# A two-level Strassen MLP kernel: blocked layout of w1 with shorter loads, eight w2 sums one superblock later, an own order for the last pair

## The chip, the cores and the metric

The kernel runs on one core of one Trainium2 chip. The metric is the device time of one execution in microseconds (us).

## The reference

A transformer MLP without biases, on 8 x 1024 tokens, all arrays float32:

```
x:  (8, 1024, 1024)     w1: (1024, 4096)     w2: (4096, 1024)
h = x @ w1
h = 0.5 * h * (1 + tanh(sqrt(2 / pi) * (h + 0.044715 * h ** 3)))
return h @ w2
```

## The kernel before, in words

**Tiling.** The 8192 tokens are worked in eight superblocks of 1024. In each, the first matrix product (x @ w1, "m1") is followed by gelu and the second (@ w2, "m2"). Both products are computed with seven block products in place of eight (Strassen's scheme in Winograd's form): each operand is cut into four blocks "11", "12", "21", "22", sums of blocks are made (`W_SUM`, products 5, 6, 7, 4; products 1, 2, 3 take raw blocks, `W_TERM`), and the seven results are added up in PSUM and by VectorE. Superblocks 0 and 1 use one level of this; superblocks 2 to 7 use two, so that each first-level product is itself made of seven second-level ones. All matmul operands are float16; all of VectorE's sums go through one helper, `tt` (line 149).

**What superblocks 0 and 1 do besides.** Superblock 0 casts w1 and w2 from float32 and keeps the float16 blocks in DRAM (`w1_d`, `w2_d`). Superblocks 0 and 1 also make the sums of weights that the later superblocks will load: the first-level sums of w1 by quads of columns (`MadeQuad.sum`, jobs "q"), their second-level sums (`MadeQuad.inner_sums`), the first-level sums of w2 (jobs "w"), and the second-level sums of w2 (`split_jobs`, jobs "p": job p26 is sum 6 of product 2; each job is two VectorE sums of 128 x 1024 and one 512 KB store into `in_d`, issued by GpSimd at line 967). Which job runs behind which tile of the second product is written out by hand in the table `FILL`, one entry for superblock 0 and one for superblock 1: the key "52" is the third tile of product 5. The order of products is 1, 2, 5, 6, 3, 7, 4. Jobs "g" are sums of gelu's outputs, jobs "x" sums of the next superblock's x, jobs "i" second-level sums (of w1's first quad in superblock 0, of x in superblock 1). The function `ahead` inside `matmul1` does the same for the first product: which w1 sums are made while which pair of column chunks is multiplied.

VectorE, like each engine, runs its instructions in program order. The adds that take a product's tile out of PSUM (`post`) stand on VectorE between these jobs.

**Superblocks 2 to 7, first product.** `matmul1_late` walks over eight pairs of column chunks, j = 0 to 7, and each pair's operands are one half of a w1 quad, `StoredHalf(0)` to `StoredHalf(7)`. A half is loaded from `w1_d` by SyncE in up to six transfers (line 295), one for each entry of `GROUPS`: operands 1 and 5; their second-level sums s1 and s5; 2 and s2; 6 and s6; 3 and s3; 7 and 4. A transfer carries 128 rows of 4096 bytes, 512 KB. For halves 3 to 7 s1 and s5 are not loaded but made by GpSimd in `make` (line 320, four sums of 128 x 512), from operands 1 and 5. Of half 0 no second-level sums of products 1, 5 and 6 are used, since products 1, 5 and 6 of pair 0 are made whole (`Pair.whole`). The halves 0 and 1 are requested in the second product of the superblock before, the others pair by pair in `matmul1_late`, three ahead. At most eight transfers are outstanding on SyncE's queue.

The order of steps in a pair is written out by hand: `PAIR` interleaves the first steps of pair j with the last steps of pair j−1 (keys with a prime), and `PAIR_FIRST` is the order for pair 0. Behind the eighth pair the primed keys of `PAIR` run by themselves; this is called the drain here. The kinds of key: `m31` is second-level product 1 of first-level product 3 (line 711, `Pair.part`, 256 columns); `h40` is half 0 of product 4, made whole (line 499, `product`, 512 columns, where `matmul1` multiplies as well); `z`, `e`, `f`, `s`, `u` are VectorE adds; `c`, `a`, `p` are copies by ScalarE; `g110` is a gelu; `d` is the difference g21 − g22 or like it (`difference`, line 518, on GpSimd, for the last pair on VectorE); `i35` is a second-level sum of x. `X_SUMS` says behind which keys of pair 1 the remaining x sums are made.

**Superblocks 2 to 7, second product.** `matmul2` uses `Inner` for each first-level product (line 1016); its w2 sums come from `in_d` and `w2_d` by SyncE. In superblocks 0 and 1 the second product's matmuls are at line 1057 (`matmuls2`).

**Layout of w1.** A w1 tile of a quad has [128 partitions, 2 halves x 4 row chunks, 256 columns]; the second-level block of a row chunk and a column chunk is a set of strided runs of 128 columns, and a chunk of columns is `[:, :, c]` with a stride.

Of the kernel before, what the change touches and what calls it, by code (L numbers as in the profile page):

```python
# [14 lines left out]
P = 128  # L15
# [19 lines left out]
m11 i35 m21 m14 a0 i55 m25 a1 m51 p0 i65 e21 m61 i15 z21  # L35
""".split()
# [16 lines left out]
def slots(table):  # L53
# [32 lines left out]
def kernel(  # L86
# [74 lines left out]
    def halves(t):  # L161
        return t.rearrange("p (h k) n -> p h (k n)", h=2)
# [22 lines left out]
    def columns(t, c, n=1):  # L185

        h, c = divmod(c, 2)
        return t[:, h * KH:(h + 1) * KH, c * P:(c + n) * P]
# [11 lines left out]
    class MadeQuad:  # L200


        def __init__(self, q, first, store):
            self.q, self.first, self.store = q, first, store
            self.raw = {b: unit(2 * KH, 2 * P) for b in BLOCKS}
            self.ops = {m: self.raw[b] for m, b in W_TERM.items()}
            if not first:
                for b in ("12", "11", "22", "21"):
                    nc.sync.dma_start(out=halves(self.raw[b]), in_=w1_at(q, term.get(b, b)))

        def load(self):

            for b, t in self.raw.items():
                k0 = (int(b[0]) - 1) * KH
                halves = t.rearrange("p (h k) n -> p k h n", h=2)
                for k in range(0, KH, 2):
                    cast_in(
                        halves[:, k:k + 2],
                        w1v[int(b[1]) - 1, :, k0 + k:k0 + k + 2, self.q * QW:(self.q + 1) * QW],
                        pool_copy,  # L220
                        view=lambda st: st.rearrange("p k (h n) -> p k h n", h=2),
                    )

        def load_cols(self, b, c, n, cast):
# [9 lines left out]
            def casts():  # L234
                for k, st, cast in staged:
                    for a in range(k // KH, (k + kn) // KH):
                        tc.keep_in_program_order(cast(
                            out=columns(self.raw[f"{a + 1}{b + 1}"], c, n),
                            in_=st[:, a * KH - k:(a + 1) * KH - k, :],
                        ))  # L240
# [3 lines left out]
        def sum(self, m, cols=None, pin=False):  # L244
            if m not in self.ops:
                self.ops[m] = self.raw["12"] if m == 7 and not self.first else unit(2 * KH, 2 * P)
# [9 lines left out]
        def inner_sums(self, m):  # L256
            t = self.ops[m].rearrange("p (h k c) (e n) -> p h k c e n", h=2, k=2, e=2)
            s = up.tile([P, 2, 4, 2, P], DT, name="u")

            def operand(b):  # L260
                if isinstance(b, int):
                    return s[:, :, list(S_SUM).index(b)]
                return t[:, :, int(b[1]) - 1, :, int(b[0]) - 1, :]
# [15 lines left out]
    class StoredHalf:  # L279


        def __init__(self, i, room=()):
# [3 lines left out]
            for ks in GROUPS:  # L286
# [7 lines left out]
                if two is not None:  # L294
                    nc.sync.dma_start(
                        out=two[:, :len(ks)].rearrange("p e n -> p (e n)"),
                        in_=w1_d[q, ks][:, h].rearrange("p e n -> p (e n)"),
                    )

        def two(self, ks):  # L300
            two = self.room.pop(0) if self.room else up.tile([P, 2, KH * 2 * P], DT, name="u")
            for e, m in enumerate(ks):
                if isinstance(m, str):
                    self.sums[int(m[1])] = two[:, e].rearrange("p (j c n) -> p j c n", j=4, c=2)
                else:
                    self.ops[m] = two[:, e].rearrange("p (k n) -> p k n", k=KH)
            return two

        def make(self):
            s = self.two(("s1", "s5")).rearrange("p e (j c n) -> p e j c n", j=4, c=2)  # L310
            t = self.both.rearrange("p e (k c r n) -> p e k c r n", k=2, c=2, r=2)

            def operand(b):
                if isinstance(b, int):
                    return s[:, :, list(S_SUM).index(b)]
                return t[:, :, int(b[1]) - 1, :, int(b[0]) - 1, :]
# [6 lines left out]
        def chunk(self, m, c):  # L323
            return self.ops[m][:, :, c % 2 * P:(c % 2 + 1) * P]

    class XOps(dict):
# [20 lines left out]
        def inner_sum(self, m, j):  # L347
# [3 lines left out]
            def operand(b):  # L351
                if isinstance(b, int):
                    return self.inner[m][:, SUMS.index(b)]
                k, t = int(b[0]) - 1, int(b[1]) - 1
# [178 lines left out]
    def matmul1(xs, sb, quads, start=None):  # L533
# [5 lines left out]
        def ahead(j):  # L539

            if j // 2 == NI // QC - 1:
                return ()
            q, second = divmod(j, 2)
            if not second:
# [5 lines left out]
            quad = quads[q + 1]  # L550
            if sb == 0:
                return [lambda m=m: quad.sum(m, pin=True) for m in SUMS] if second else ()
# [116 lines left out]
    class Pair:  # L669
# [21 lines left out]
        def part(self, m, i):  # L691
# [8 lines left out]
            for k in range(2):  # L700
                if i in S_TERM:
                    r, o = (int(d) - 1 for d in S_TERM[i])
                    w = ops[:, 2 * o + k, r * P:(r + 1) * P]
                else:
                    w = self.source.sums[m][:, list(S_SUM).index(i), k, :]
                if i in W_TERM:
                    o, t = (int(d) - 1 for d in W_TERM[i])
                    x = xs[m][:, 2 * o + k, t * HT // 2:(t + 1) * HT // 2]
# [56 lines left out]
    def matmul1_late(xs, sb, quads, g):  # L765
# [10 lines left out]
        for j in range(n + 1):  # L776
            if MADE_HALF <= j + 1 < n:
                quads[j + 1].make()
            if j < n:
                quads += [StoredHalf(i) for i in range(len(quads), min(j + 3, n))]  # L780
                now = Pair(j, quads[j], xs, g)
            for key in PAIR if j else PAIR_FIRST:
# [4 lines left out]
                elif j < n:  # L787
                    now.run(key)
# [3 lines left out]
            if j == n:  # L792
                break
# [400 lines left out]
```

## Time and profile before

| | us |
|---|---|
| median of three timed runs | 1492.52 |
| the three | 1492.61, 1492.52, 1486.17 |
| the profiled execution's own time | 1490.02 |
| its span in the profile | 1488.2 |
| TensorE busy in it | 1460.1 |
| VectorE busy | 1263.1 |
| ScalarE busy | 612.2 |
| GpSimd busy | 457.1 |

The stages in the profiled execution, read from the timeline of TensorE, in us from the start of the span: superblock 0's first product ends at about 113 and its second at 215; superblock 1's end at 313 and 410; superblock 2's at 500 and 592; each later superblock takes about 180; the span ends at 1488.

How to read it: PE is TensorE, DVE VectorE, ACT ScalarE, POOL GpSimd, SP SyncE. A row of a timeline has the start, the duration, the engine, the line, the operation with its output and inputs by the program's names and their shape, how many of them in a row, and in brackets the idle time before the first of them and what ended it. Names such as `u`, `gc`, `g` and `tmp` are pools of tiles: `u` holds weights and x, `g` and `gc` gelu's outputs and their sums, `tmp` partial results in float32, `ps` PSUM banks. A row of waits has the engine's line, the releaser, and the total, the count and the longest wait. Durations of matmuls overlap, so that two in a row start closer together than they last.

### The profile page before, as it was taken

Reading aid. Unit: us, or ns where it says so; the run is one execution under the profiler, and the core shown is the slowest. Engines: PE = TensorE matmul, PEld = TensorE weight load, DVE = VectorE, ACT = ScalarE, POOL = GpSimd, SP = SyncE. Lnnn points to the kernel's source line nnn. Section 1 sums busy time; section 2 is a strip of 40 time slices with the busy share of each in tenths; the row PEclk is TensorE's granted clock in tenths of the full one; section 3 lists DMA queues with packets and bytes.
Section 4 is the critical chain, followed back from the end, with each engine's and each line's share of the span. In section 5 each row is a group of like instructions: output and inputs, shape, how many; then the busy total and the mean of one; then the engine's idle time right before and its main releaser. Section 6 shows DMA issues by size and latency. Waiting matters only on the chain.

```text
span 1488.2 us, 28427 instructions
## 1 busy us (share of the span) xinstructions
PE 1460.1 (98%) x10635; PEld 1038.2 (70%) x10635; DVE 1263.1 (85%) x2226; ACT 612.2 (41%) x1226; POOL 457.1 (31%) x473
## 2 busy tenths in 40 slices
PE   8999989999999999999999999999999999999998
PEld 4444434444477788778876788777886778867787
DVE  5657648757789999999998999999999999999987
ACT  5566016631067411663126721366213762156510
POOL 1542222212346012560026501264012731136111
PEclk9999999999999999999999999999999999999999
DMA  9999998887899999999999999999999999997896
GB/s 325 342 352 399 269 362 315 276 264 247 345 342 236 325 325 374 370 233 364 301 370 341 226 372 306 360 349 226 380 332 351 321 276 337 348 377 237 311 303 214
DMA packets 205706, 472.69 MB, mean 318 GB/s; under 512 B 75648, under 2 KB 80768, under 8 KB 204672
## 3 DMA queue, kind: packets, MB, share of 16 engines
q1 hardware_dynamic: 177632, 373.35, 73.7%
q0 software_dynamic: 27936, 97.53, 21.9%
q8 instruction: 83, 1.36, 0.4%
q14 instruction: 55, 0.45, 0.1%
HBM read 370.15 MB, written 115.34 MB: 326 GB/s over the span
## 4 chain that ended last, share of the span: by engine, by line
PE 81%; DVE 7%; DMA 7%; issue 2%; SPq 2%; POOL 1%; POOLq 0%; DVEq 0%
PE ps L1016 32%; PE ps L499 21%; PE ps L711 17%; PE ps L1057 10%; DMA u<-w_d 5%; DVE tmp L149 2%; DVE ps L149 2%; SPq L173 2%; DVE u L149 2%; DMA g<-w_d 2%; DVE gc L149 1%; PE ps L432 1%; POOL u L320 1%; DMA gc<-in_w_dram 1%; POOL xb L474 0%
## 5 line engine op out<-in xcount | busy, mean ns | idle before, releaser
L149 DVE TENSOR_TENSOR tmp<-tmp,ps 128x256 f32<-128x256 f32 (+1 forms) x582 | 312.9, 555 | 94.1 <-PE ps L499 38.6
L499 PE MATMUL ps<-u 128*128 128x512 f16 x1552 | 364.2, 379 | 2.7 <-DVE u L149 1.8
L176 ACT COPY tmp<-ps 128x512 f32<-128x512 f32 (+1 forms) x398 | 208.7, 541 | 301.2 <-PE ps L1057 148.1
L149 DVE TENSOR_TENSOR ps<-tmp,ps 128x256 f32<-128x256 f32 x720 | 293.2, 425 | 34.2 <-PE ps L711 24.7
L711 PEld LDWEIGHTS <-u 128*128 128x128 f16 x2688 | 263.3, 98 | 80.8 <-DMA u<-w_d 6.2
L1016 PE MATMUL ps<-u,gc 128*128 128x256 f16 x2592 | 290.8, 273 | 0.0
L1016 PEld LDWEIGHTS <-gc 128*128 128x128 f16 x2592 | 253.6, 98 | 29.4
L149 DVE TENSOR_TENSOR u<-u 128x2048 f16<-128x2048 f16 (+3 forms) x320 | 231.9, 768 | 31.1 <-DMA u<-w_d 15.1
L499 PEld LDWEIGHTS <-u 128*128 128x128 f16 x1552 | 151.6, 98 | 151.0 <-issue 5.4
L512 ACT ACTIVATE g<-ps 128x512 f16<-128x512 f32 x326 | 190.0, 594 | 118.5 <-PE ps L711 71.2
L711 PE MATMUL ps<-u 128*128 128x256 f16 x1520 | 229.6, 274 | 0.0
L1016 PE MATMUL ps<-u,g 128*128 128x256 f16 x2016 | 227.9, 273 | 0.0
L176 ACT COPY u<-ps 128x512 f32<-128x512 f32 (+1 forms) x134 | 77.9, 586 | 353.2 <-PE ps L1016 345.6
L826 POOL DMA_DIRECT2D out_dram<-u x70 | 63.8, 955 | 488.1 <-DVE u L149 251.4
L1016 PEld LDWEIGHTS <-g 128*128 128x128 f16 x2016 | 197.3, 98 | 22.8
L711 PE MATMUL ps<-gc,u 128*128 128x256 f16 x1168 | 194.9, 274 | 9.4 <-DMA u<-w_d 5.1
L149 DVE TENSOR_TENSOR u<-u,ps 128x512 f32<-128x512 f32 x216 | 147.8, 684 | 37.1 <-PE ps L1016 29.0
L1057 PE MATMUL ps<-u,g 128*128 128x512 f16 x768 | 168.1, 381 | 3.8 <-DVE tmp L149 3.8
L518 POOL TENSOR_TENSOR g<-g,g 128x1024 f16<-128x1024 f16 x42 | 89.2, 2124 | 202.8 <-ACT g L512 202.8
L320 POOL TENSOR_TENSOR u<-u 128x512 f16<-128x512 f16 x120 | 136.2, 1156 | 35.7 <-DMA u<-w_d 25.5
L1057 PEld LDWEIGHTS <-g 128*128 128x128 f16 x768 | 75.5, 98 | 95.8 <-issue 6.3
L512 ACT ACTIVATE g<-tmp 128x512 f16<-128x512 f32 x186 | 117.0, 630 | 43.7 <-DVE tmp L149 43.3
(54 smaller groups left out, 898.5 us busy)
## 6 DMA issues: line engine op xcount, KB each, us to landing
u<-w_d SPq DMA_DIRECT2D x365, 512.0 KB, 8.8
u<-in_d SPq DMA_DIRECT2D x168, 512.0 KB, 8.2
out_dram<-u POOLq DMA_DIRECT2D x70, 512.0 KB, 11.1
gc<-in_w_dram SPq DMA_DIRECT2D x48, 512.0 KB, 5.9
g<-w_d SPq DMA_DIRECT2D x45, 512.0 KB, 13.1
w_d<-u POOLq DMA_DIRECT2D x40, 512.0 KB, 6.1
w_d<-u SPq DMA_DIRECT2D x32, 512.0 KB, 8.9
in_d<-u POOLq DMA_DIRECT2D x28, 512.0 KB, 7.2
```

The source lines that it names most:

```text
L149: i = nc.vector.tensor_tensor(out=out, in0=in0, in1=in1, op=op)
L173: return tc.keep_in_program_order(nc.sync.dma_start(out=out, in_=in_, **kw))
L176: tc.keep_in_program_order(nc.scalar.copy(out=out, in_=in_))
L320: nc.gpsimd.tensor_tensor(out=operand(j), in0=operand(u), in1=operand(v), op=op)
L432: tc.keep_in_program_order(nc.tensor.matmul(bank[:, cols], lhsT=w[:, k, :], rhs=self.xs.blocks[f"{a}{r}"][:, k, cols], start=r == 1 and k ...
L499: tc.keep_in_program_order(nc.tensor.matmul(bank, lhsT=w, rhs=x, start=first and k == 0, stop=k == n - 1, skip_group_check=not first,))
L512: gelu_last[0] = nc.scalar.activation(out=out, in_=src, func=GELU)
L518: tc.keep_in_program_order(engine.tensor_tensor(out=g["21"][:, cs], in0=g["11"][:, cs], in1=g["21"][:, cs], op=SUB,))
L711: tc.keep_in_program_order(nc.tensor.matmul(out, lhsT=w, rhs=x, start=first and k == 0, stop=k == 1, skip_group_check=not first,))
L826: return nc.gpsimd.dma_start(out=rows, in_=src, **kw)
L1016: tc.keep_in_program_order(nc.tensor.matmul(bank[:, i * OH // 2:(i + 1) * OH // 2], lhsT=t[:, c, i * P:(i + 1) * P], rhs=self.y[j][:, c, : ...
L1057: tc.keep_in_program_order(nc.tensor.matmul(pair(bank), lhsT=a[:, c, :], rhs=chunks(pieces[c // QC])[:, :, c % QC, :], start=(first and c ...
```

## The change

Three things are changed.

1. **Layout and shorter loads.** w1's tiles hold the column chunks outermost, so each second-level block is a contiguous run of 256 elements, and the blocks are ordered so that the fourth block of a tile's last operand comes last. Second-level products use three raw blocks ("11", "12", "22") and four sums; the block that stands last is only needed for making sums. Where a transfer carries an operand's sums and the operand itself, the operand now stands second (`GROUPS`), and the transfer leaves out its last 512 bytes of each row of 4096, so 64 KB of 512 KB. This holds for two transfers of half 0, four each of halves 1 and 2 and three each of halves 3 to 7: 25 in each of superblocks 2 to 7, 150 in all, 9.8 MB. The order of x's blocks in the inner contraction is turned around to match.
2. **Jobs.** The eight jobs that make the second-level w2 sums of products 2 and 3 (p25, p26, p27, p24, p35, p36, p37, p34) go from superblock 0's second product to superblock 1's. At the end of superblock 0's second product the x sums come ahead of the first quad's sums (q5, q6, q7, q4), which start at the second tile of product 4. `ahead` in superblock 1 is rearranged: the second-level sums of product 6 are made one quad later. The x sum i3 of superblock 1 is left to superblock 2, which makes it as the later superblocks do.
3. **Drain.** The drain runs the same keys as before in an order of its own, `PAIR_LAST`.

The core of the diff (the edits in `columns`, `raw`, `load_cols` and the views of sums that follow from the layout are left out):

```diff
-GROUPS = ((1, 5), ("s1", "s5"), (2, "s2"), (6, "s6"), (3, "s3"), (7, 4))
+GROUPS = ((1, 5), ("s1", "s5"), ("s2", 2), ("s6", 6), ("s3", 3), (7, 4))
...
+PAIR_LAST = """
+e20 m26 z62 z53 m67 z22 z63 m31 m54 m63 m35 z64 s0 p1 m22 m64 m27 m23 z31 e30 s1 h70 m36 m32 h71
+u0 z32 g220 m33 g110 z23 u1 g120 m37 h40 g221 e31 z24 g210 z33 h41 z34 g211 m24 g111 d m34 g121
 """.split()
...
     slots("""10:g60 p15;11:g61 p16;12:g62 p17;13:g63
     ;20:g50 w50 w51;21:g51 w52;22:w53 g52;23:g53 p14
-    ;50:w60 w61;51:w62 w63;52:g30 g31 p25;53:g32 g33 p26
-    ;60:w70 w71 p27;61:w72 w73 p24;62:w40 w41;63:w42 w43
-    ;30:p35;31:p36;32:p37;33:p34
-    ;72:q5;73:q6 x5;40:q7 q4 x7;41:i2 i6 x6;42:i3 i1 x3
-    ;43:i5""".replace("\n    ", "")),
+    ;50:w60 w61;51:w62 w63;52:g30 g31;53:g32 g33
+    ;60:w70 w71;61:w72 w73;62:w40 w41;63:w42 w43
+    ;73:x5;40:x7 x6;41:x3 q5;42:q6 q7 q4
+    ;43:i2 i3 i1 i5""".replace("\n    ", "")),
     slots("""10:g60 w50;11:g61 w51;12:g62 w52;13:g63 w53
     ;20:g50 p55;21:g51 p56;22:g52 p57;23:g53 p54
-    ;50:w60 w61;51:w62 w63;52:g30 g31;53:g32 g33
-    ;60:p65 w70;61:p66 w71;62:p67 w72;63:p64 w73
-    ;30:w40 w41;31:w42 w43;32:p75;33:p76
+    ;50:w60 w61;51:w62 w63;52:g30 g31 p25;53:g32 g33 p26
+    ;60:p65 w70;61:p66 w71;62:p67 w72 p27;63:p64 w73 p24
+    ;30:w40 w41;31:w42 w43;32:p75 p35;33:p76 p36
     ;70:p77 p74;71:x5 p45;72:x7 p46;73:x6 p47
-    ;40:p44;41:x3;42:i2;43:i3""".replace("\n    ", "")),
+    ;40:p44 p37;41:x3 p34;42:i2""".replace("\n    ", "")),
...
                 if two is not None:
+                    n = 2 * KH * 2 * P
+                    if ks == (1, 5):
+                        unread = 0 < i < MADE_HALF
+                    else:
+                        unread = ks[1] in (2, 3) or ks[1] == 6 and i
+                    if unread:
+                        n -= 2 * P
                     nc.sync.dma_start(
-                        out=two[:, :len(ks)].rearrange("p e n -> p (e n)"),
-                        in_=w1_d[q, ks][:, h].rearrange("p e n -> p (e n)"),
+                        out=two.rearrange("p e n -> p (e n)")[:, :n],
+                        in_=w1_d[q, ks][:, h].rearrange("p e n -> p (e n)")[:, :n],
                     )
...
-            jobs = [lambda m=m: quad.sum(m, pin=True) for m in ((7, 4) if second else (5, 6))]
-            inner = (2, 3) if second else (6,)
-            if q == 0:
-                inner += (5,) if second else (1,)
-            return jobs + [lambda m=m: quad.inner_sums(m) for m in inner]
+            sums = [] if last else [(q + 1, m) for m in ((7, 4) if second else (5, 6))]
+            inner = [] if last or not second else [(q + 1, 2), (q + 1, 3)]
+            if not second:
+                inner.append((q, 6))
+            if q == 1:
+                inner.append((q, 5 if second else 1))
+            return [lambda at=at, m=m: quads[at].sum(m, pin=True) for at, m in sums] + [
+                lambda at=at, m=m: quads[at].inner_sums(m) for at, m in inner
+            ]
...
+            if j == n:
+                for key in PAIR_LAST:
+                    last.run(key)
+                break
             for key in PAIR if j else PAIR_FIRST:
```

More of the change, by code (lines that the diff above doesn't have):

```diff
@@ L204, in __init__ @@
             self.q, self.first, self.store = q, first, store
[L205 removed]
+            self.raw = {b: unit(QC, KH * P) for b in BLOCKS}
             self.ops = {m: self.raw[b] for m, b in W_TERM.items()}
@@ L245, in sum @@
             if m not in self.ops:
-                self.ops[m] = self.raw["12"] if m == 7 and not self.first else unit(2 * KH, 2 * P)
+                self.ops[m] = self.raw["12"] if m == 7 and not self.first else unit(QC, KH * P)
             u, op, v = W_SUM[m]
@@ L539, in ahead @@
         def ahead(j):
-            if j // 2 == NI // QC - 1:
-                return ()
             q, second = divmod(j, 2)
-            if not second:
+            last = q == NI // QC - 1
+            if not second and not last:
                 quad = MadeQuad(q + 1, sb == 0, sb == 1)
@@ L549, in ahead @@
                     quads[q].keep_raw()
[L550 removed]
             if sb == 0:
[L552 to L557 removed]
+                return [lambda m=m: quads[q + 1].sum(m, pin=True) for m in SUMS] if second and not last else ()
+            sums = [] if last else [(q + 1, m) for m in ((7, 4) if second else (5, 6))]
[7 more added lines that the diff above has]
+            ]
         nxt = {}
```

37 lines of the change are left out of this document (18 added, 19 removed).

## The prediction

> **What bounds the kernel now.** I read the page's busy shares first, then the list of what TensorE waited for, and then timelines of the stretches where those waits lie.
>
> ```profile
> span 1488.2 us, 28427 instructions
> PE 1460.1 (98%) x10635; PEld 1038.2 (70%) x10635; DVE 1263.1 (85%) x2226; ACT 612.2 (41%) x1226; POOL 457.1 (31%) x473
> ```
> ```profile
> PE ps L711 <- DMA u<-w_d: 5.1, 4, 2.2
> PE ps L711 <- POOL u L320: 4.3, 3, 2.6
> PE ps L1057 <- DVE tmp L149: 3.8, 1, 3.8
> PE ps L499 <- DVE u L149: 1.8, 1, 1.8
> ```
>
> TensorE is busy for 98% of the span. The change leaves the number of matmuls and their shapes alone, so it can only win or lose in the 28 us of idle time, and in what the clock loses after an idle stretch. The four rows say where most of it is. L711 is the second-level part of a pair at the start of superblocks 3 to 7. L1057 and the L499 row are single places at the seam from superblock 0 to 1. The sum is made against the profiled execution: 1490.0 us, with 1488.2 of span and 1.8 around it. The three timed runs have a median of 1492.5, 2.5 above it, and the lowest is 1486.2, so about 0.5% (7.5 us) is what a measurement of this kernel can tell from no change.
>
> **Part 1, the seam from superblock 0 to 1.** The next views are VectorE's and TensorE's timelines there, and a window's row (time, busy of PE, PEld, DVE, ACT, POOL, then clock, DMA share, GB/s).
>
> ```profile
> 207.90 1.23 DVE L149 TENSOR_TENSOR u<-u 128x2048 f16<-128x2048 f16 x1 [15.06 <-DMA u<-w_d]
> 209.04 0.68 DVE L149 TENSOR_TENSOR tmp<-tmp,ps 128x512 f32<-128x512 f32 x1
> ```
> ```profile
> 209.77 5.16 PE L1057 MATMUL ps<-u,g 128*128 128x512 f16 x16 [3.85 <-DVE tmp L149]
> 223.68 2.53 PE L499 MATMUL ps<-u 128*128 128x512 f16 x11 [1.84 <-DVE u L149]
> ```
> ```profile
> 209.70:213.20 3.50, 3.43 (x9) 1.23 (x9) 3.50 (x5) 0.00 (x0) 1.65 (x3) 0.54 1.06 407
> ```
>
> VectorE works in order. It stands for 15.06 us before job q5, the first quad sum, because raw w1 has not landed. Behind q5 is the add of product 7's last tile, which frees a PSUM bank for product 4, so TensorE stands for 3.85 us. For the 3.50 us after that the granted clock is 0.54, which loses (1 − 0.54) × 3.5 = 1.6 us. The other sums of that list, queued behind it, then hold back the x sum x3, and TensorE waits another 1.84 us. In all 7.3 us.
>
> The changed order puts x5, x7, x6 and x3 ahead of q5 and q5 behind the adds of product 7, so neither wait on VectorE has the late load in front of it. It also takes the eight jobs p25 to p27, p24 and p35 to p37, p34 out of superblock 0, that is eight stores of 512 KB. In the window DMA is full (share 1.06), so the raw loads land earlier too. By the row at 590 further down, 512 KB takes 1.26 us of full DMA, so eight are 10 us of DMA time. What would be late next is q5 itself: of the sums that follow it superblock 1 needs only the first ones soon. I take the whole 7.3. If q5 is as late as now, part of the 1.84 and some wait on q6 come back, which I bound at −4; no more than 8 is to be had.
>
> **Part 2, the start of superblock 2.** The eight jobs go to superblock 1: 16 sums and eight stores. The window of its second product:
>
> ```profile
> 313.00:412.00 99.00, 99.00 (x461) 45.00 (x460) 68.17 (x88) 11.99 (x21) 27.40 (x50) 1.00 0.83 278
> ```
>
> TensorE has no stall there and VectorE is idle for 31 of 99 us, against 16 × 0.72 = 11.5 us for the sums, by this form's row,
>
> ```profile
> L149 DVE TENSOR_TENSOR u<-u 128x1024 f16<-128x1024 f16 x68 | 46.1, 720 | 1.4 <-ACT u L237 1.0 <-PE ps L432 0.3
> ```
>
> so the sums cost nothing where they stand. But x inner sum i3 also leaves for superblock 2, and the built program shows that the first loads of half 0 and half 1 now reuse tiles whose last reader is such a store. SyncE issues in order, so every load behind waits too.
>
> ```profile
> DMA to landing us min/median/max: 3.0/7.2/14.0
> ```
>
> That is for these stores (line 967). Before, those loads had waited for TensorE only, and the start of superblock 2 had no stall at all, with its loads far ahead. After, I expect it to look like the starts of superblocks 3 to 7. There a collision can be read. VectorE at the start of superblock 2 and of superblock 3, and GpSimd at both:
>
> ```profile
> 425.69 0.42 DVE L149 TENSOR_TENSOR gc<-u,gc 128x512 f16<-128x512 f16 x1
> ```
> ```profile
> 426.00 2.12 POOL L518 TENSOR_TENSOR g<-g,g 128x1024 f16<-128x1024 f16 x1 [13.10 <-ACT g L512]
> ```
> ```profile
> 602.58 2.29 DVE L149 TENSOR_TENSOR gc<-u,gc 128x512 f16<-128x512 f16 x1
> ```
> ```profile
> 602.48 2.11 POOL L518 TENSOR_TENSOR g<-g,g 128x1024 f16<-128x1024 f16 x1 [12.10 <-ACT g L512]
> ```
>
> The same x sum takes 0.42 us when it starts ahead of GpSimd's difference and 2.29 us when it starts 0.1 us behind it, and the adds that free PSUM stand behind that. With i34 to i37 now made in superblock 2's second pair as well, I expect the collision there: 2.29 − 0.42 = 1.87, so +1.9. Bounds: 0 if VectorE comes first, +5 if a load comes that much late (two thirds of a median landing).
>
> The Trainium skill, page "SBUF — State Buffer", section "Who interferes with whom", says that a VectorE instruction with two SBUF inputs and a GpSimd instruction that reads SBUF exclude each other, and that the one issued first wins. The four rows agree. By it the term is 1.9 or nothing, and the forecast 1478 or 1476.
>
> **Part 3, the starts of superblocks 3 to 7.** These are TensorE's waits in five stretches, in this order: 592 to 620 (two rows), 772 to 800 (two), 953 to 980 (two), 1133 to 1160 (three), 1312 to 1330 (one).
>
> ```profile
> PE ps L711 <- DMA u<-w_d: 1.2, 1, 1.2
> PE ps L711 <- DVE tmp L149: 0.6, 1, 0.6
> ...
> PE ps L711 <- POOL u L320: 2.6, 1, 2.6
> PE ps L711 <- DVE tmp L149: 0.2, 1, 0.2
> ...
> PE ps L711 <- DMA u<-w_d: 2.2, 1, 2.2
> PE ps L711 <- POOL u L320: 1.1, 1, 1.1
> ...
> PE ps L711 <- DMA u<-w_d: 1.5, 1, 1.5
> PE ps L711 <- POOL u L320: 0.6, 1, 0.6
> PE ps L711 <- DVE tmp L149: 0.4, 1, 0.4
> ...
> PE ps L711 <- DVE tmp L149: 1.7, 1, 1.7
> ```
> ```profile
> 590.00:600.00 10.00, 9.86 (x69) 6.68 (x69) 9.96 (x28) 4.72 (x10) 0.38 (x1) 1.00 1.03 416
> 592.00:620.00 28.00, 26.01 (x185) 18.60 (x183) 25.66 (x63) 16.37 (x34) 10.56 (x11) 0.94 1.03 382
> ```
>
> The trimmed loads leave out 64 KB of 512 KB. At 416 GB/s with DMA full, 512 KB is 1.26 us and 64 KB is 0.158 us. Ahead of half 2's second load stand 2 trims of half 0, 4 of half 1 and 1 of half 2: 7 × 0.158 = 1.1 us. Ahead of half 3's first load, which is the input of GpSimd's sums at line 320, stand 10: 1.6 us earlier.
>
> The sums at line 320 then start up to 1.6 us earlier. Of the waits on them 2.6 loses 1.6, 1.1 and 0.6 go: −3.3. The waits on the load are another matter. DMA and DVE together make 1.8, 1.9 and 1.7 us in the first, fourth and fifth stretch, whatever the DMA part is: that is about the 1.87 of the collision, which holds TensorE anyway. So a load that lands 1.1 us earlier takes nothing off there; what shows as DMA now would show as DVE. Only the third stretch, with 2.2, is above it: −0.3. So the term is −3.6. Bounds: 0, if GpSimd's earlier start is lost again or superblock 4, which has no collision now, gets one; and −7, if the clock comes back too: the row at 592 has 0.94 over 28 us, 1.7 us lost, and superblock 4's start has as much.
>
> The Trainium skill, page "TensorE: Matmul & The Clock Gate", section "What's actually happening", has the clock fall to half after an idle window of about 3.4 us. At 209.70 that agrees, behind 3.85 us; at 592 the clock falls with no wait over 1.2 us, so there the measured row decides. By the page the 1.7 us of superblocks 3 and 4 do not hang on these waits and stay, 1478; by the row they may go with the waits, 1475.
>
> **Part 4, the drains.** The last pair of each of superblocks 2 to 7 runs alone, in the order it has when the next pair is interleaved.
>
> ```profile
> 675.99 0.38 PE L711 MATMUL ps<-u 128*128 128x256 f16 x2
> 676.52 1.02 PE L499 MATMUL ps<-u 128*128 128x512 f16 x4 [0.15 <-DVE tmp L149]
> ```
> ```profile
> 678.81 0.38 PE L711 MATMUL ps<-gc,u 128*128 128x256 f16 x2
> 679.02 0.38 PE L711 MATMUL ps<-u 128*128 128x256 f16 x2
> 679.39 1.02 PE L499 MATMUL ps<-u 128*128 128x512 f16 x4
> ```
>
> Two matmuls of 256 columns pass in 0.21 to 0.22 us (678.81 to 679.02). So TensorE loses 0.31 us ahead of 676.52 and 0.16 ahead of 679.39: 0.47 us, and six times that is 2.8. The new order puts four second-level parts (m31, m54, m63, m35) and m22, m64 between a column of adds and the product that needs it, so I take all of it, −2.8. Bounds: −3.6 with the smaller gaps beside these, and +1 if a stall comes at another add, since VectorE is nearly full there.
>
> **Layout.** Inner sums read contiguous runs of 256 where they read strided ones; the counts and sizes of instructions stay. I cost it at 0, from −1 to +1: VectorE and GpSimd have fixed times by form here. The two more inner sums that superblock 1 gets lie beside its slack.
>
> **Sum.** 1490.0 − 7.3 + 1.9 − 3.6 − 2.8 = 1478.2, given as 1478.
>
> **The rivals.** (A) Slower: the trimmed rows are not carried as one packet.
>
> ```profile
> q1 hardware_dynamic: 177632, 373.35, 73.7%
> ```
>
> From the row at 590, 128 rows of 4096 B on 16 engines in 1.26 us are 157 ns each; this row gives 16 × 1488.2 × 0.737 / 177632 = 99 ns for a mean of 2102 B. The line through both has a fixed part of about 37 ns a packet (an estimate). If 3584 is cut into 2048, 1024 and 512, each engine pays 2 × 8 × 37 = 0.59 us more a load, 0.43 after the saving. Ten such loads put half 3's first load 4.3 us later at six starts that have no slack then: 1490.0 − 7.3 + 1.9 − 2.8 + 26 = 1508. It decides as soon as a trimmed load takes over 1.26 us of full DMA, and is slower than before from 1.4 us a start. For it: no packet of this size has run. Against: nothing in the rows makes 4096 special. Chance 0.1.
>
> (B) The stores at the seam into superblock 2 hold SyncE so long that the load for half 2 is the last to land: +6 to +9 in place of +1.9, so 1482 to 1485. For it: landings up to 14.0 us, and DMA full. Chance 0.17.
>
> (C) The trims are worth nothing, because GpSimd's sums and the collision set the starts whatever lands: −3.6 falls away, 1482. Chance 0.2.
>
> (D) The change does not do what it says at the drains, the new order stalling as often elsewhere: −2.8 falls away, 1481. Chance 0.13.
>
> **How the numbers follow.** My forecast has 0.4, and its own range, from the bounds of the four parts, is 1472 to 1483. The whole range 1470 to 1489 takes in B, C and D, alone and most pairs of them, and leaves out A and the corner where all goes wrong. Faster by over 0.5% means below 1482.5 against the profiled run: nearly all of the forecast (0.38 of 0.4), somewhat over half of C (0.12), which lies just below that bound, two thirds of D (0.09) and a third of B (0.06): 0.65. The rest of these four, with their pairs and worse bounds, is within 0.5%: 0.24. Slower: A, and a hundredth for a seam that costs more than all gains: 0.11.
>
> **What would show it.** Right: no idle before a 128x2048 sum around 205, clock 1.00 there; the wait on L149 of L1057 gone; a stall of about 1.9 us on DVE in superblock 2 near 425; the POOL L320 waits at 1 us in all; DVE in place of DMA in the starts; drains of six times 0.1. The page's DMA total should be 9.8 MB lower (150 trimmed loads). Wrong: a DMA wait over 3 us at 412 to 440, L320 waits as before, or packets of q1 growing in number.

## The result, and the profile after

The changed kernel takes 1480.28 us (median of six, 1479.40 to 1483.45), the kernel before 1490.91 (median of six by now, 1486.17 to 1492.61). The ratio is 0.9938, with a 95% interval of 0.9919 to 0.9958: 9 us less by the ratio, 10.6 by the medians. The profiled executions are 1483.45 and 1490.02, so the traces below account for 6.6 us.

The page after, its busy shares, DMA total and SyncE's queue, and then the list of what TensorE waited for:

```profile
span 1481.7 us, 28425 instructions
PE 1457.0 (98%) x10635; PEld 1039.1 (70%) x10635; DVE 1264.3 (85%) x2226; ACT 611.1 (41%) x1226; POOL 454.9 (31%) x473
...
DMA packets 205706, 462.86 MB, mean 312 GB/s; under 512 B 75648, under 2 KB 80768, under 8 KB 204672
...
q1 hardware_dynamic: 177632, 363.52, 73.1%
```
```profile
PE ps L723 <- DVE tmp L152: 6.1, 4, 2.0
PE ps L723 <- DMA u<-w_d: 5.9, 4, 2.2
PE ps L723 <- POOL u L330: 4.3, 3, 2.9
...
PE ps L723 <- DMA g<-w_d: 1.1, 1, 1.1
```

Line numbers have moved: L723 is the former L711, L330 the former L320, L152 the helper `tt`. The matmuls are the same 10635. The two single places (L1057 on an add, L499 on x3) are gone. What is left behind the kernel's start is all at L723, and its waits sum to more than before (17.4 against 12.3 us), because superblock 2 has joined in. The 9.83 MB are off SyncE's queue with the same number of packets.

The lists of waits leave out what the clock loses, so I use one more measure: for each matmul the time to the next one's start, less the step of its form in an unbroken stretch (0.2156 us for 512 columns, 0.109 for 256), summed over a place. In every profile but one the execution's time is 1450.9 to 1451.5 plus the sum of its row's five places (1451.8 in the last but one), so little else moves. Each ratio is against runs of the kernel before from the same session, whose medians lie between 1490.56 and 1491.33. In us:

| kernel | time, median of all | ratio to before (95%) | kernel start | seam 0 to 1 and superblock 1 | start of 2 | starts of 3 to 7 | six drains | profiled time |
|---|---|---|---|---|---|---|---|---|
| before | 1490.91 | | 6.1 | 7.7 | 0.4 | 20.1 | 4.6 | 1490.02 |
| changed | 1480.28 | 0.9938 (0.9919–0.9958) | 6.0 | 0.2 | 6.0 | 17.2 | 2.9 | 1483.45 |
| changed, again | 1481.03 | 0.9935 (0.9914–0.9956) | 5.6 | 0.2 | 4.3 | 18.4 | 2.9 | 1482.35 |
| seam's order alone | 1485.47 | 0.9977 (0.9956–0.9998) | 6.0 | 1.4 | 0.1 | 20.2 | 4.6 | 1483.40 |
| drain alone | 1489.62 | 0.9986 (0.9965–1.0007) | 5.5 | 11.3 | 0.4 | 18.1 | 2.9 | 1489.68 |
| changed, full loads | 1485.76 | 0.9961 (0.9946–0.9975) | 5.7 | 0.2 | 5.4 | 19.8 | 2.6 | 1484.76 |
| changed, w2 jobs back | 1480.09 | 0.9928 (0.9909–0.9947) | 6.3 | 2.0 | 4.0 | 14.4 | 2.6 | 1480.17 |
| changed, w2 jobs halved | 1478.52 | 0.9918 (0.9904–0.9931) | 5.8 | 0.2 | 4.0 | 17.1 | 2.6 | 1480.65 |
| changed, x sum early | 1475.63 | 0.9894 (0.9879–0.9909) | 5.4 | 0.2 | 3.2 | 10.5 | 2.9 | 1473.21 |
| halved and early | 1466.77 | 0.9832 (0.9817–0.9846) | 6.2 | 0.2 | 0.5 | 6.6 | 2.6 | 1467.10 |
| before, x sum early | 1490.14 | 0.9988 (0.9973–1.0003) | 6.0 | 10.3 | 0.4 | 19.0 | 4.6 | 1492.09 |
| halved and early, full loads | 1470.67 | 0.9870 (0.9851–0.9890) | 6.3 | 0.2 | 0.5 | 13.4 | 2.6 | 1474.13 |

One profile is one execution. The same code has 7.7, 11.3 and 10.3 us at the seam in its three profiles (before, drain alone, before with x sum early), and 17.2 and 18.4 at the starts of superblocks 3 to 7 in the two profiles of the changed kernel, so a single cell says little below about 3 us unless its rows are read too.

The seam, TensorE's timeline and the window of the same stretch:

```profile
202.82 6.42 PE L1071 MATMUL ps<-u,g 128*128 128x512 f16 x29
209.08 17.21 PE L509 MATMUL ps<-u 128*128 128x512 f16 x79
```
```profile
203.00:226.00 23.00, 23.00 (x108) 10.44 (x107) 18.56 (x34) 10.26 (x19) 8.72 (x14) 1.00 1.01 394
```

No idle time and a clock of 1.00. VectorE still waits for the raw w1, but less, and with nothing urgent behind it:

```profile
205.01 1.23 DVE L152 TENSOR_TENSOR u<-u 128x2048 f16<-128x2048 f16 x1 [3.94 <-DMA u<-w_d]
206.60 9.35 DVE L152 TENSOR_TENSOR u<-u 128x2048 f16<-128x2048 f16 x19 [0.36 <-DMA u<-w_d]
```

The start of superblock 2 has two stalls where there were none, TensorE first and then VectorE and GpSimd at the first of them:

```profile
421.13 0.39 PE L723 MATMUL ps<-gc,u 128*128 128x256 f16 x2 [2.25 <-DMA u<-w_d]
435.28 0.39 PE L723 MATMUL ps<-gc,u 128*128 128x256 f16 x2 [2.88 <-POOL u L330]
```
```profile
418.76 2.37 DVE L152 TENSOR_TENSOR gc<-u,gc 128x512 f16<-128x512 f16 x1
```
```profile
418.73 2.12 POOL L528 TENSOR_TENSOR g<-g,g 128x1024 f16<-128x1024 f16 x1 [13.52 <-ACT g L522]
```

The collision has come to superblock 2: GpSimd starts 0.03 us ahead and the x sum takes 2.37 us. It ends at 421.13, just when the load lands, so the wait is put down to DMA while both were late. The second stall is GpSimd's sums of half 3, which begin only here:

```profile
431.73 4.60 POOL L330 TENSOR_TENSOR u<-u 128x512 f16<-128x512 f16 x4 [9.61 <-PE ps L509]
```

The row names TensorE, which was done at 431.53; in the trace a load of w1 landed at 431.61, 0.12 us before the sums began, and in the second profile of this kernel at 429.51, 0.13 us before.

### The profile page after: what moved, and what is told of

It reads as the page before. It is cut to its first block, busy times and chain, and to the rows that moved or that the text cites. A ratio compares the mean times of both kernels' runs of the same rounds, so it can differ in the third digit from the quotient of the medians.

```text
span 1481.7 us, 28425 instructions
## 1 busy us (share of the span) xinstructions
PE 1457.0 (98%) x10635; PEld 1039.1 (70%) x10635; DVE 1264.3 (85%) x2226; ACT 611.1 (41%) x1226; POOL 454.9 (31%) x473
## 3 DMA queue, kind: packets, MB, share of 16 engines
q1 hardware_dynamic: 177632, 363.52, 73.1%
## 4 chain that ended last, share of the span: by engine, by line
PE 91%; DVE 4%; DMA 3%; POOL 1%; issue 1%; ACT 0%; SPq 0%; DVEq 0%
PE ps L1030 34%; PE ps L509 22%; PE ps L723 20%; PE ps L1071 13%; DMA u<-w_d 3%; DVE gc L152 1%; DVE u L152 1%; PE ps L442 1%; DVE tmp L152 1%; POOL u L330 1%; DVE ps L152 1%; PE ps L419 0%; DMA u<-in_x_dram 0%; PE ps L377 0%; ACT u L179 0%
## 5 line engine op out<-in xcount | busy, mean ns | idle before, releaser
L152 DVE TENSOR_TENSOR tmp<-tmp,ps 128x256 f32<-128x256 f32 (+1 forms) x582 | 311.0, 553 | 90.1 <-PE ps L509 39.5
L152 DVE TENSOR_TENSOR ps<-tmp,ps 128x256 f32<-128x256 f32 x720 | 292.2, 425 | 33.8 <-PE ps L723 24.3
L723 PEld LDWEIGHTS <-u 128*128 128x128 f16 x2688 | 262.5, 98 | 80.4 <-DMA u<-w_d 7.5
L152 DVE TENSOR_TENSOR u<-u 128x512 f16<-128x512 f16 (+3 forms) x316 | 231.2, 774 | 27.5 <-DMA w_d<-u 11.4
L723 PE MATMUL ps<-u 128*128 128x256 f16 x1456 | 220.2, 273 | 0.0
L723 PE MATMUL ps<-gc,u 128*128 128x256 f16 x1232 | 202.7, 273 | 10.4 <-DMA u<-w_d 5.9
L152 DVE TENSOR_TENSOR u<-u,ps 128x512 f32<-128x512 f32 x216 | 147.4, 682 | 36.6 <-PE ps L1030 27.4
L330 POOL TENSOR_TENSOR u<-u 128x512 f16<-128x512 f16 x120 | 136.3, 1158 | 33.5 <-DMA u<-w_d 13.3
## 6 DMA issues: line engine op xcount, KB each, us to landing
u<-w_d SPq DMA_DIRECT2D x125, 448.0 KB, 10.1
```

What stands on the lines that cost most here:

```text
L152: i = nc.vector.tensor_tensor(out=out, in0=in0, in1=in1, op=op)
L330: nc.gpsimd.tensor_tensor(out=operand(j), in0=operand(u), in1=operand(v), op=op)
L723: tc.keep_in_program_order(nc.tensor.matmul(out, lhsT=w, rhs=x, start=first and k == 0, stop=k == 1, skip_group_check=not first,))
```

## The experiments

**The changed kernel again.**

> The changed kernel as it is, for a second profile beside the others of this chip. In its first profile the start of superblock 2 cost 5.6 us of TensorE time over full rate (2.2 on a w1 load, 2.9 on GpSimd's sums of half 3, 0.4 on an earlier load) against 0.4 in the kernel before, and that execution was 3 us longer than the median of six. Theory (the sb2 start varies from execution to execution with the landing of loads): median near 1480, and a profile whose time is near 1480 shows about 2.5 us there. Rival (the cost is fixed, the 3 us lie elsewhere): 5 to 6 us at the start of superblock 2 again.

The profiled execution took 1482.35 us and lost 4.3 us at superblock 2, with 1.8 on a load and 1.9 on GpSimd's sums. The cost varies by 1.7 us between two profiles, but it stays well above the 1.9 of the prediction. So it is not fixed, as the rival had it, and the 2.5 us of the theory were not seen either; neither profile was of an execution near the median.

**The seam's order alone.** The edit to the kernel before:

```diff
-    ;72:q5;73:q6 x5;40:q7 q4 x7;41:i2 i6 x6;42:i3 i1 x3
-    ;43:i5""".replace("\n    ", "")),
+    ;73:x5;40:x7 x6;41:x3 q5;42:q6 q7 q4
+    ;43:i2 i6 i3 i1 i5""".replace("\n    ", "")),
```

> The kernel before with one edit: in superblock 0's last tiles the x sums x5, x7, x6, x3 go ahead of q5, and q5, q6, q7, q4 behind tile 41. The eight w2 jobs stay in superblock 0, the loads and the drain stay. Theory (it is VectorE's order alone): no wait at line 1057 and none on x3, 7.3 to 7.6 us less than before, ratio 0.995. Rival (the stores of the eight jobs keep the raw w1 late, so the queue behind q5 moves the wait to the first products of superblock 1): 3 to 5 us less, with a new wait between 215 and 235 us.

```profile
209.06 20.02 PE L499 MATMUL ps<-u 128*128 128x512 f16 x92
230.10 2.10 PE L499 MATMUL ps<-u 128*128 128x512 f16 x9 [1.02 <-ACT tmp L176]
```

The stall of 3.85 us, the half clock and the wait on x3 are gone by the order on VectorE alone. A new wait of 1.02 us at 230 takes its place in superblock 1, where the rival had one; its row names a copy of ScalarE, so that late raw w1 makes it is not shown. By the table the seam goes from 7.7 to 1.4 us. By the times the edit is worth 3.4 us by the ratio, inside the rival's 3 to 5, and 5.6 by the medians, between the two.

**The drain alone.** To the kernel before, `PAIR_LAST` and its use in the last turn of the loop:

```diff
-            for key in PAIR if j else PAIR_FIRST:
+            for key in (PAIR_LAST if j == n else ()):
+                last.run(key)
+            for key in (() if j == n else PAIR if j else PAIR_FIRST):
```

> The kernel before with one edit: the last pair of superblocks 2 to 7 runs in the new order of its own. Theory: each drain loses 0.27 us instead of about 0.7, so 2.4 to 2.8 us less than before, ratio 0.998, and nothing else moves. Rival (what the drain gains is given back at the next wait on a load, since the second product's loads do not come earlier): no change within 0.5 us, with new waits behind the drains.

The six drains go from 4.6 to 2.9 us, five of them from 0.76 or more to about 0.44, and the sixth, in superblock 4, from 0.83 to 0.75. Nothing is given back behind them. The ratio of 0.9986 is 2 us, inside an interval that takes in none; the rows carry this verdict, not the time.

This run also shows the seam in a worse case of the same code:

```profile
212.70 5.58 PE L1063 MATMUL ps<-u,g 128*128 128x512 f16 x16 [7.43 <-DVE tmp L153]
226.60 5.77 PE L503 MATMUL ps<-u 128*128 128x512 f16 x26 [1.42 <-DVE u L153]
```

The wait is 7.43 us where it was 3.85, since the raw w1 landed later. With 0.2 us left there in the changed kernel, the seam's term is worth from 7.5 to 11.1 us, by the execution.

**Full loads.** The changed kernel without

```diff
-                    if unread:
-                        n -= 2 * P
```

> The changed kernel with every load at its full 512 KB (layout, jobs and drain as changed). Theory of the prediction: the trims are worth 3.6 us, by earlier sums on GpSimd, so about 1484, with waits on GpSimd's sums of 2 to 3 us at superblocks 4 to 6 back and DMA volume back at 472.7 MB; at the start of superblock 2 another 1 to 2 us. Rival (the collision on VectorE and GpSimd's sums set the starts whatever lands): within 1 us of 1480.

It is 4.7 to 5.5 us slower than the changed kernel by the medians (1485.76 against 1481.03 and 1480.28), and 0.9961 against 0.9938 by the ratio, 3.4 us. The prediction had 3.6. The runs of the two kernels in the same session hardly overlap (1482.17 to 1487.99 against 1476.92 to 1482.35). The waits:

```profile
PE ps L721 <- DMA u<-w_d: 8.5, 4, 2.3
PE ps L721 <- DVE tmp L152: 4.1, 2, 2.0
PE ps L721 <- POOL u L328: 3.2, 3, 1.1
```

In the changed kernel DMA has 5.9 and DVE 6.1: what the trims take from the wait on loads does reappear as a wait on VectorE. Summed over the starts of superblocks 3 to 7, the waits at this line are 12.4 us with full loads and 11.8 and 12.1 in the two profiles of the changed kernel, so there is hardly less waiting; the clock falls twice in these starts with full loads and once in each of the others. The profiles differ by 1.3 and 2.4 us only, so how the 4.7 to 5.5 of the medians come about is not shown.

**The eight w2 jobs back in superblock 0.** To the changed kernel; in superblock 1's table the same eight are taken out:

```diff
-    ;50:w60 w61;51:w62 w63;52:g30 g31;53:g32 g33
-    ;60:w70 w71;61:w72 w73;62:w40 w41;63:w42 w43
+    ;50:w60 w61;51:w62 w63;52:g30 g31 p25;53:g32 g33 p26
+    ;60:w70 w71 p27;61:w72 w73 p24;62:w40 w41;63:w42 w43
+    ;30:p35;31:p36;32:p37;33:p34
```

> The changed kernel with the eight w2 jobs (p25 to p27, p24, p35 to p37, p34) put back at their old places in superblock 0; the new order of x and quad sums, the shorter loads, the drain and the moved x sum i3 stay. The start of superblock 2 cost 6.0 and 4.3 us in two profiles of the changed kernel, 0.4 in the kernel before. Theory (the stores of these jobs make it, by their DMA time and by SyncE waiting for their landing): 0.3 to 2.2 us there (2.2 with the collision of the x sum and GpSimd's difference), 1 to 1.5 us new in superblock 1 as in the kernel with the seam's order alone, so about 1478. Rival (it is the x sum i3 that moved into superblock 2's second pair): 4 to 6 us there as now, about 1482.

**Four of them back.** The first part is superblock 0's table, the others superblock 1's:

```diff
-    ;50:w60 w61;51:w62 w63;52:g30 g31;53:g32 g33
-    ;60:w70 w71;61:w72 w73;62:w40 w41;63:w42 w43
+    ;50:w60 w61;51:w62 w63;52:g30 g31 p35;53:g32 g33 p36
+    ;60:w70 w71 p37;61:w72 w73 p34;62:w40 w41;63:w42 w43
...
-    ;30:w40 w41;31:w42 w43;32:p75 p35;33:p76 p36
+    ;30:w40 w41;31:w42 w43;32:p75;33:p76
...
-    ;40:p44 p37;41:x3 p34;42:i2""".replace("\n    ", "")),
+    ;40:p44;41:x3;42:i2""".replace("\n    ", "")),
```

> The changed kernel with product 3's four jobs in superblock 0, at the places that product 2's had (52, 53, 60, 61), and product 2's four in superblock 1 as changed: four stores each, none of the moved ones in the last stretch before either seam. Theory: no new wait in superblock 1 (the stores are over well before the raw w1 is asked for) and 0.3 to 2.5 us at the start of superblock 2, so 1476 to 1478. Rival: superblock 2's start does not depend on these stores, 4 to 6 us there, about 1481.

With all eight back, superblock 1 begins with waits on raw w1, which the changed kernel has not:

```profile
209.93 1.90 PE L510 MATMUL ps<-u 128*128 128x512 f16 x8 [0.43 <-DMA u<-w_d]
212.92 19.38 PE L510 MATMUL ps<-u 128*128 128x512 f16 x89 [1.08 <-DMA u<-w_d]
```

With four back there is none. In both the start of superblock 2 loses 4.0 us, so the stores are not the whole of it. The kernel with four back shows what is left there, TensorE's row and the windows across it:

```profile
420.93 0.47 PE L723 MATMUL ps<-u 128*128 128x256 f16 x2 [1.97 <-DVE tmp L152]
```
```profile
416.00:421.00 5.00, 3.03 (x25) 2.19 (x23) 5.00 (x10) 3.72 (x8) 2.85 (x3) 1.00 1.02 398
421.00:424.50 3.50, 3.50 (x18) 2.51 (x18) 2.32 (x6) 0.86 (x2) 3.41 (x5) 0.51 1.17 329
```

It is the collision, 1.97 us, as predicted, and behind it 3.5 us at a clock of 0.51, which lose another 1.7. The waits on the load and on GpSimd's sums of half 3 are gone, and these sums begin 8 to 10 us earlier than in the changed kernel (431.73 there, 429.64 in its second profile), so those were the stores:

```profile
421.55 4.63 POOL L330 TENSOR_TENSOR u<-u 128x512 f16<-128x512 f16 x4
```

Neither theory had the number (both said at most 2.5). The rival to the first, that it is the moved x sum i3, had the number and part of the cause: the collision is at superblock 2 in all five profiles that make i3 there with i64 in its old place, and in none of the three that make i3 in superblock 1. The layout differs between the two groups as well, so i3 alone is not shown. The times hardly move: 1480.09 with eight back and 1478.52 with four, against 1480.28 and 1481.03, with intervals that overlap.

**The x sum early.** The changed kernel with

```diff
-    "g121'": ("i64",),
+    "p0": ("i64",),
```

> The changed kernel with one edit: in the second pair of superblocks 2 to 7 the x sum i64 is made behind step p0 instead of behind the last step, so that it is over before GpSimd's difference starts. Theory of the collision (the sum takes 2.3 us instead of 0.42 when GpSimd's difference starts first, and TensorE waits 2 us for the adds behind it): no VectorE instruction of 2.3 us in this place, the waits of 1.9 to 2.0 us on VectorE at superblocks 4, 6 and 7 gone, 0.3 to 1.5 us of waits on loads in their place, 3 to 6 us less than the changed kernel, 1475 to 1477. Rival (the loads would have held TensorE as long): waits on the load of 1.5 to 2 us in the same places, within 1 us of 1480.5.

This tests the collision by itself. The group of these sums in the changed kernel, and in this one:

```profile
L152 DVE TENSOR_TENSOR gc<-u,gc 128x512 f16<-128x512 f16 x48 | 28.0, 614 | 0.0
```
```profile
L152 DVE TENSOR_TENSOR gc<-u,gc 128x512 f16<-128x512 f16 x48 | 18.5, 416 | 0.0
```

The same 48 sums take 9.5 us less: five times 1.9, superblocks 2, 3, 4, 6 and 7 of that profile. TensorE's waits then:

```profile
PE ps L723 <- DMA u<-w_d: 4.1, 3, 1.9
PE ps L723 <- POOL u L330: 3.2, 3, 2.0
PE ps L723 <- ACT g L522: 1.6, 2, 0.8
```

No wait on VectorE is left at L723, and the time is 4.7 to 5.4 us below the changed kernel's medians. The theory stands, though the waits that are left on loads and GpSimd's sums reach 2.0 us, above the 1.5 it gave.

**Both edits**, the four jobs back and the x sum early, in one kernel.

> The two edits before this one together: product 3's w2 jobs in superblock 0 and the x sum i64 early. If both theories hold their gains add up, since they lie at different places but for the start of superblock 2: 1471 to 1474. If the start of superblock 2 was the collision all along, the two together give no more than the larger of them.

1466.77 us, below the 1471 to 1474 that the sum of the two gains gave, and 13.5 to 14.3 below the changed kernel. The start of superblock 2 explains part: with four jobs back it lost 4.0 us to the collision and the clock, with the sum early 3.2 to loads and what follows them, with both 0.5. Each edit alone only let the other cause show. The starts of 3 to 7 also go from 10.5 to 6.6 against the x sum early alone; that is one profile each, and what makes it is not shown.

```profile
PE ps L723 <- DMA u<-w_d: 1.7, 2, 1.1
...
PE ps L723 <- POOL u L330: 0.6, 1, 0.6
```

**The x sum early, in the kernel before**, the same two lines as above.

> The kernel before with one edit, the x sum i64 behind step p0 instead of behind the pair's last step. The changed kernel got 10 us less at its starts of superblocks 2 to 7 from this edit. Theory (the collision holds TensorE about 2 us at superblocks 3, 5, 6 and 7 in the kernel before too, but there the loads without trims stand right behind it): the starts of 3 to 7 go from 20 us over full rate to 13 to 16, 4 to 7 us less than before, mostly at superblock 7, with waits on loads of 1 to 2.5 us left in the others. Rival (the collision only hides itself behind loads that are as late): within 1.5 us of before.

The collision is gone there too (46 such sums with a mean of 418 ns against 582), and the time is the same within its interval. At superblock 4 and 5 its waits are

```profile
PE ps L711 <- POOL u L320: 3.8, 1, 3.8
...
969.17 0.51 PE L711 MATMUL ps<-gc,u 128*128 128x256 f16 x2 [3.62 <-DMA u<-w_d]
```

Only superblock 7 gets better by all of the collision's 1.9 us (2.7 to 0.8); superblocks 3 and 6 gain 1.5 and 0.8, and 4 and 5 lose 1.2 and 1.8. By the time the rival holds. Its reason, that the loads are as late, fits these two rows, but the size of the loads is not enough for it: the next kernel has full loads too, and there the starts cost 13.4 us, not 19.0. What else in the change it takes (the layout with the order of transfers, the jobs, the drain) was not tried apart.

**The fastest kernel with full loads**, without the two lines that trim, as above.

> The fastest kernel so far (the changed one with product 3's w2 jobs in superblock 0 and i64 early, 1466.8) with all loads at their full 512 KB. It asks what the trims are worth once nothing else holds the starts. Theory (the collision had covered the trims, each start then gains up to the 1.1 to 1.6 us by which the loads are earlier, and the clock with it): 6 to 10 us slower, 1473 to 1477, with waits on loads of 1 to 2.5 us at most of the starts. Rival (the trims stay worth the 1.5 to 5 us that they are beside the collision): 1468 to 1471.

1470.67: 3.9 us slower by the medians, 5.7 by the ratios (0.9870 against 0.9832). The waits at L721 on loads and on GpSimd's sums come back at 1.3 us or less each:

```profile
PE ps L721 <- POOL u L328: 4.5, 4, 1.2
PE ps L721 <- DMA u<-w_d: 4.3, 4, 1.3
```

By the median it is the rival's case, by the ratio it lies just above; the profile alone, with 6.8 us more at the starts of 3 to 7, would have been the theory's. The trims are worth some 3 to 6 us with the collision and without it. Without it they do shorten the waits: on loads from 4.3 to 1.7 us, on GpSimd's sums from 4.5 to 0.6.

## Why the prediction was right, and where its steps were off

The forecast of 1478 lies 2.3 us from the median, the ratio of 0.9938 on the profiled 1490.0 gives 1480.8. The sign, the size and the four places were right; the four terms were off in both directions. That the total came out so near is in part luck. The sum of the four terms was −11.8; in the two profiles of the changed kernel the four places give −6.5 and −7.0 against the profile that the sum started from. The medians moved by more, 10.6 and 10.1, and one reason on record is that this profile had a cheap seam: 7.7 us, where two later profiles of the same code have 11.3 and 10.3.

- **Seam, −7.3.** Measured −7.5 in the two profiles, of which the order alone made 6.3. Mechanism and size were right. What the prediction did not see is that the wait before varies with the landing of raw w1, 3.85, 6.44 and 7.43 us in three profiles of the same code. Its doubt about q5 was sound: with the stores left in superblock 0 waits of 1.0 to 1.5 us appear in superblock 1; taking out four of them is enough to remove that.
- **Start of superblock 2, +1.9.** Measured +5.6 and +3.9. This term was mis-sized. The collision came as predicted; it is worth 1.97 by its row where nothing else is late, and in the changed kernel a load that lands as the x sum ends is as late. Left out were GpSimd's sums of half 3, late with their load behind the moved stores (2.9 and 1.9 us). The clock stays whole here in both profiles of the changed kernel; it falls, for 1.7 us, where the jobs are put back, which is why that start still loses 4.0. The bound of +5 was too low too. The part that went with the stores is rival B's mechanism, at a smaller price than its +6 to +9: in that stretch of superblock 1 the DMA share goes from 0.83 to 0.95, and putting four jobs back removes those two waits.

```profile
313.00:412.00 99.00, 98.75 (x473) 45.92 (x471) 77.08 (x113) 12.59 (x23) 31.45 (x57) 1.00 0.95 314
```

- **Starts of 3 to 7, −3.6.** The table has −2.9 and −1.7 by the profiles, and full loads against trimmed ones 3.4 us by the ratio: the size is near, but the mechanism that gave it, 3.3 us less waiting on GpSimd's sums, is not what the profiles show. Those waits fell from 4.3 us to 1.4 and 2.4 at these starts, but kernels with full loads have anything from 0.2 (the drain alone) to 6.8 (before, x sum early) on the same sums, so one profile does not tell. And all waits at these starts together go only from 12.3 to 11.8 and 12.1. The sign "L320 waits at 1 us in all" did not come: with superblock 2 they are 4.3 in both. What the prediction said of the loads, that what shows as DMA would show as DVE, held for the other waits too: in the changed kernel superblocks 4, 6 and 7 show 2.0, 1.9 and 2.0 us on VectorE and nothing on loads, and with four jobs back each of the five starts has 1.8 to 2.0 on VectorE and nothing else. Most of what was gained here is clock: it no longer falls at superblocks 3 and 4, 1.7 us each, as the bound of −7 allowed. Given back: superblock 4, which had no collision before, got one (the bound named it), and at superblock 7 the clock now falls behind the stall, 1.7 us that were not lost before:

```profile
1314.40:1316.90 2.50, 0.48 (x5) 0.28 (x3) 2.50 (x3) 1.24 (x4) 1.85 (x1) 1.00 1.03 410
1316.90:1321.10 4.20, 4.18 (x24) 3.12 (x24) 3.05 (x8) 1.24 (x3) 3.20 (x3) 0.59 1.02 403
```

- **Drains, −2.8.** Measured 0.33 each, so −2.0 for six, as in five profiles; in four others, the two of the changed kernel among them, one of the six drains loses 0.3 to 0.4 more, and it is −1.7. The two gaps that were counted did go, but the new order leaves one of 0.15 and one of 0.12 us at other adds, where I took none. In a drain of the changed kernel the starts lie 0.37 and 0.34 us apart there, in place of 0.22:

```profile
849.33 0.38 PE L723 MATMUL ps<-u 128*128 128x256 f16 x2
849.70 0.38 PE L723 MATMUL ps<-gc,u 128*128 128x256 f16 x2
...
851.43 0.38 PE L723 MATMUL ps<-u 128*128 128x256 f16 x2
851.77 1.02 PE L509 MATMUL ps<-u 128*128 128x512 f16 x4
```

- **Rival A** is excluded. SyncE's queue has the same 177632 packets before and after for 9.83 MB less, and in the trace a packet of 3584 bytes took a median of 140 ns, one of 4096 bytes 159.
- **Rival C**, the trims worth nothing, is excluded by the times of both kernels with full loads. Its reasoning, that the collision sets the starts, was half true: moving the x sum gave 5 us in the changed kernel and nothing that can be measured in the kernel before.
- **Rival D**, the drains stalling as often elsewhere, is excluded by the drains' own rows: 1.7 to 2.0 of the 2.8 us came.
- **Layout, 0.** Busy VectorE time is 1264.3 against 1263.1, and nothing in the list of waits points to it. It was not tried alone.

The Trainium skill's page "SBUF — State Buffer", section "Who interferes with whom", has the instruction issued first win. The trace agrees down to 0.03 us (418.73 against 418.76, the x sum at 2.37 us), and 0.42 us returns as soon as the order is turned. The Trainium skill's page "TensorE: Matmul & The Clock Gate", section "What's actually happening", has half clock after an idle window of about 3.4 us. Here it followed waits of 1.97 and 2.04 us, and a wait of 2.03 us at superblock 4 was not followed by it.

The traces show what decides, and that the stretch need not be idle throughout. In all twelve profiles the changes of the clock lie whole multiples of 3.41 us apart, so an execution can be cut into such stretches, and the clock is halved for the next one according to how full the last one was. With each matmul counted at its unbroken step, TensorE was at work for at most 0.37 of the stretch ahead of each of the 21 falls, and for at least 0.40 of every other stretch at full clock. The stall at superblock 7 lies whole in one stretch (first two rows), the one at superblock 4, as long, is shared between two (last two):

```profile
1314.23:1317.64 3.41, 1.37 (x13) 1.08 (x12) 3.41 (x6) 1.41 (x4) 2.02 (x1) 1.00 1.02 402
1317.64:1321.05 3.41, 3.41 (x18) 2.45 (x17) 2.26 (x6) 1.19 (x3) 3.15 (x3) 0.50 1.02 409
...
778.34:781.75 3.41, 1.71 (x15) 1.37 (x14) 3.41 (x6) 2.47 (x6) 2.44 (x3) 1.00 0.88 340
781.75:785.17 3.42, 3.09 (x28) 2.67 (x28) 3.35 (x10) 1.46 (x3) 0.94 (x2) 1.00 1.02 395
```

So a fall needs some 2.1 us of lost time within one stretch, in one wait or several; this is also why the clock fell at superblock 3 in the kernel before with no wait over 1.2 us. Where the stretches begin differs from execution to execution, so in a sum a stall of 2 us is worth a range of 0 to 1.7 us of clock behind it.

## What to carry to other kernels

When several things are late at one place, the list of waits names the last only; the sum at the place staying the same while its parts change (1.8, 1.9, 1.7 us here) is the sign of a second cause behind it. Such causes have to be taken away together: the x sum early gained nothing in the kernel before, 5 us in the changed one and, with four stores moved as well, 14. And work moved out of one full stretch of DMA should be spread to where DMA has room, not to the next seam: with the x sum early, four of the eight jobs in either superblock took 1466.8 us where eight in the later one took 1475.6. (Eight in the earlier one with the x sum early was not tried.)

## What the runs showed of the hardware that was not expected

The clock halved for 3.41 us behind stalls of only 2 us and not behind others as long, by where they lay in stretches of 3.41 us, so an idle stretch of 2 us on TensorE can cost 3.7 us. And 0.03 to 0.2 us in the order of two engines was worth 1.9 us four to six times in an execution: a 128x512 sum of VectorE took 2.2 to 2.4 us whenever GpSimd's 128x1024 difference had started before it, and 0.42 otherwise.
